# Where the raw weights of the next head pair are fetched to, and when the triangular inverse runs, in a hybrid RWKV-7 / FoX layer

## The chip, the cores and the metric

The kernel runs on one core of a Trainium2 chip. The metric is the device time of one execution in microseconds; the median of three executions of the kernel before is 1712.96 us (1705.19, 1712.96 and 1714.62 us).

Of the core's engines the text uses these names: PE is the matrix engine (PEld its weight loads), DVE the vector engine, ACT the scalar engine, POOL GpSimd, and SP the engine whose queue issues nearly all DMA transfers. Each engine works its queue in the order in which it stands.

## The reference, cut to what matters

One layer over 2048 positions of width 1024: a norm, one input projection, two branches (an RWKV-7 recurrence over 8 heads of 64, and attention with a forget gate over 8 heads), a gate, an output projection and a final norm.

```
h = rmsnorm(x, norm_g);  p = h @ w_in                      # 2048x1024 @ 1024x4232
p_rw, p_fox, gate = p[:, :1664], p[:, 1664:3208], p[:, 3208:]
# RWKV: r, k, v are 512 columns each; token shift, decay w, rate a, normalised kk
step:  sa    = state @ (-kk_t)
       state = state * w_t + sa (x) (kk_t * a_t) + v_t (x) k_t
       y_t   = state @ r_t
# FoX: softmax(q k^T / 8 + c_i - c_j, causal) @ v, with c the running sum of log_sigmoid(f)
y = concat(y_rw, y_fox) * silu(gate);  x = x + y @ w_out;  out = rmsnorm(x, final_g)
```

The kernel computes the recurrence in chunks of 64 positions: inside a chunk it needs the inverse of a unit lower triangular 64x64 matrix for each chunk and head.

## The kernel before, in words

**Stages.** Four blocks of 512 positions of x are loaded, normalised, transposed and split into a high and a low half-precision part (`load_x_block`). Then the main loop (L671 to L696) takes the RWKV heads in four pairs `p`, each over four blocks `b`. Attention, the chunk recurrence and the output projection follow; they are only started while the last projections run, and the change does not touch their code.

**A pair and a block.** For each block the loop projects r, k and v (`proj_T`, 24 matmuls of 512 columns each, L254), shifts them in time (`shifted`), and calls `prep`, a long chain over all engines: decay by a scan (L487), normalisation through PE (`ss`, L95 and L96), `rs`, `nk`, `k`, `th`, the pair of tiles `bk` and `ga` (L532 and L527), the matmuls `pb` and `pk` that multiply them (L541, L544), and masks that leave the triangular matrices in `mab`. Most results are stored to DRAM for the recurrence. After `prep`, `step(1)` writes one portion of the fillers.

**Fillers.** The attention projections (`fox_proj`, L332) and the gate projections (`gate_proj`, L254 with `pj_g`) do not depend on the pair loop. They are written as a generator in seven groups, f0, f1, f2, g0, g3, g6, f3, of which one portion is written after each block. PE uses them when the chain of `prep` is not ready.

**Weights.** A group of three 128-column tiles is fetched raw (32-bit, 512 KB each, L199) into tiles of the tag `wr`, of which there are three for the pairs and the fillers together. `prep_w` then takes the largest magnitude on DVE (`am`, L200), crosses partitions with two small PE operations (`over_partitions`, tile `px`), scales the tile on DVE (L216), rounds it on ACT (L218) and takes the remainder on POOL (L219). The rounded tiles of a pair (`wh_r`, `wl_r`) exist three times, so those of the next pair can only be written once the last block's projections have used the old ones. In the kernel before, `rw_weights(p + 1)`, fetch and conversion together, is written ahead of the projections of block 2 (`P_W` = 2).

**The inverse.** `inverse(p - 1, ...)` (L574) inverts the pair's triangular matrices on DVE: transposes into a tile `mu`, 60 small dependent operations on `tv` (L588, L590), transposes into `z` (32x64 per partition, 8 KB) and `ta` (same buffer as `mu`). `inverse_end` (L601) adds the off-diagonal blocks by small PE matmuls (L607, L615) with copies on ACT, and stores `z` to DRAM (L619). The first half is written after block 1 of the next pair (`P_INV` = 1), the second after block 2 (`P_END` = 2).

**Order.** The tile framework fixes the order in each engine's queue when the kernel is built: it plans all instructions on a modelled time line, in the order in which they are written where several could go, and an instruction written later may stand earlier in a queue if its inputs and its buffer are free earlier. On the chip that order then holds, whatever the real times are.

Of the kernel before, what the change touches and what calls it, by code (L numbers as in the profile page):

```python
# [9 lines left out]
F32 = mybir.dt.float32  # L10
# [20 lines left out]
NEG = -1e30  # L31
LN16 = math.log(16.0)
GS = 2048.0
P_W, P_INV, P_END = 2, 1, 2
N_A, N_B = 5, 20
VS = 2.0 ** -20
HR = ((0, 64), (64, 128))
# [2 lines left out]
def hymba_body(tc, x, norm_g, w_in, rw_mu, rw_w_up, rw_w0, rw_a_up, rw_a0, rw_k_k, rw_k_a, rw_r_k,  # L40
# [7 lines left out]
    with ctx:  # L48
# [140 lines left out]
            ts(isc[:, 0:n].bitcast(I32), e, 23, ALU.logical_shift_left)  # L189
            return sc  # L190

        def prep_w(n, offs, tag, outs, iall):

            nt = len(offs)
            am = wp.tile([128, 3, KT, 2], F32, name="am_" + n, tag="am")
            wrs = []
            for i, c0 in enumerate(offs):
                wr = wp.tile([128, KT, 128], F32, name=f"wr_{n}{i}", tag="wr", bufs=3)
                nc.sync.dma_start(wr, w_in[0, :, c0:c0 + 128].rearrange("(k p) n -> p k n", p=128))  # L199
                nc.vector.tensor_reduce(am[:, i].rearrange("q k g -> q (k g)"),  # L200
                                        wr.rearrange("q k (g c) -> q (k g) c", c=64), AX.X, ALU.max,
                                        apply_absolute_value=True)
                wrs.append(wr)
            a3 = am[:, 0:nt].rearrange("q i k g -> q (i k) g")
            nc.vector.tensor_tensor(a3, a3, gabx[:, 0:nt * KT].unsqueeze(2).to_broadcast([128, nt * KT, 2]), ALU.mult)
            mx = wp.tile([128, 6], F32, name="mx_" + n, tag="mx")
            nc.vector.tensor_reduce(mx[:, 0:2 * nt].rearrange("q (i g) -> q i g", g=2),
                                    am[:, 0:nt].rearrange("q i k g -> q i g k"), AX.X, ALU.max)
            ma = over_partitions(n, mx[:, 0:2 * nt], 2 * nt, wp, tag)
            sc = pow2_scale(n, ma, 2 * nt, wp, iall, tag)  # L210
            for i in range(nt):
                nc.vector.tensor_tensor(am[:, i], g_c.unsqueeze(2).to_broadcast([128, KT, 2]),
                                        sc[:, 2 * i:2 * i + 2].unsqueeze(1).to_broadcast([128, KT, 2]), ALU.mult)
            for i, (wr, (oh, ol)) in enumerate(zip(wrs, outs)):
                w3 = wr.rearrange("q k (g c) -> q (k g) c", c=64)
                nc.vector.tensor_tensor(w3, w3, am[:, i].rearrange("q k g -> q (k g)").unsqueeze(2)  # L216
                                        .to_broadcast([128, 2 * KT, 64]), ALU.mult)
                nc.scalar.activation(oh, wr, AF.Copy)  # L218
                nc.gpsimd.tensor_tensor(ol, wr, oh, ALU.subtract)  # L219

        def load_tiles(name, offs):

            iall = wp.tile([128, 6], F32, name="ia_" + name, tag="ia", bufs=2)
            ws = [(wp.tile([128, KT, 128], F16, name=f"wh_{name}{i}", tag="wh", bufs=3),
                   wp.tile([128, KT, 128], F16, name=f"wl_{name}{i}", tag="wl", bufs=3)) for i in range(len(offs))]
            prep_w(name, offs, "r", ws, iall)
            return ws, iall

        def load_w(name, offs, extra=None):

            wh = wp.tile([128, KT, 386], F16, name="fh_" + name, tag="fh", bufs=2)
            wl = wp.tile([128, KT, 386], F16, name="fl_" + name, tag="fl", bufs=2)
            iall = wp.tile([128, 6], F32, name="ja_" + name, tag="ja", bufs=2)
            cs = [slice(128 * i, 128 * i + 128) for i in range(len(offs))]
            prep_w(name, offs, "f", [(wh[:, :, c], wl[:, :, c]) for c in cs], iall)
            if extra is not None:
                for dst, src in ((wh, extra[0]), (wl, extra[1])):
                    nc.gpsimd.tensor_copy(dst[:, :, 384:386], src)
            return wh, wl, iall
# [143 lines left out]
        def group_w(i, fw):  # L383
            kind, n = groups[i]
            if kind == "f":
                c, fs = OFF_FOX + n * 128, slice(2 * n, 2 * n + 2)
                return load_w(f"f{n}", [c + j * 512 for j in range(3)], (fw[0][:, :, fs], fw[1][:, :, fs]))
            return load_w(f"g{n}", [OFF_GATE + (n + j) * 128 for j in range(min(3, 8 - n))])

        def fillers():  # L390

# [19 lines left out]
        with c1:  # L411
# [162 lines left out]
            def inverse(p, mab):  # L574

                mu = T(f"mu{p}", "mu", 1, (128, 32, 32))
                tv = T(f"tv{p}", "tv", 1, (128, 32, 32))
                nc.vector.transpose(mu.rearrange("q t s -> q (t s)"), mab[:, 0:32, :].rearrange("q t u -> q (t u)"))
                for q0 in (32, 96):
                    nc.vector.transpose(mu[q0:q0 + 32].rearrange("q t s -> q (t s)"),  # L580
                                        mab[q0:q0 + 32, 32:64, :].rearrange("q t u -> q (t u)"))
                nc.gpsimd.tensor_copy(tv, mu)
                nc.gpsimd.memset(tv.rearrange("q t j -> q (t j)")[:, 0:1024:33], 1.0)
                tm = T(f"tm{p}", "tm", 1, (128, 256))
                for s_ in range(1, 31):
                    r = 31 - s_
                    w = tm[:, 0:r * s_].rearrange("q (t j) -> q t j", j=s_)
                    nc.vector.tensor_tensor(w, mu[:, s_ + 1:32, s_:s_ + 1].to_broadcast([128, r, s_]),  # L588
                                            tv[:, s_:s_ + 1, 0:s_].to_broadcast([128, r, s_]), ALU.mult)
                    nc.vector.tensor_tensor(tv[:, s_ + 1:32, 0:s_], tv[:, s_ + 1:32, 0:s_], w, ALU.add)  # L590

                z = T(f"z{p}", "z", 1, (128, 32, 64))
                ta = T(f"ta{p}", "mu", 1, (128, 32, 32))
                nc.vector.transpose(z[:, :, 0:32].rearrange("q u t -> q t u"), tv)
                for q0 in (32, 96):
                    nc.vector.transpose(z[q0:q0 + 32, :, 32:64].rearrange("q u t -> q t u"), tv[q0:q0 + 32])
                    nc.gpsimd.memset(z[q0:q0 + 32, :, 0:32], 0.0)
                nc.vector.transpose(ta.rearrange("q u j -> q j u"), tv.rearrange("q t j -> q j t"))
                return partial(inverse_end, p, mab, z, ta)
# [19 lines left out]
                nc.sync.dma_start(d_z[p], z)  # L619

            load_x_block(0, sp, ps_r)
            whl, wll, iscl = load_w("l", [1536])
            with nc.allow_non_contiguous_dma("small parameter columns"):
                mu_c = pcol(rw_mu, 13, "mu_c")
            omu_c = derived("omu_c", mu_c, -1.0, ALU.mult, 1.0, ALU.add)
            sml, sol = mix_scales("l", iscl, 1, mu_c[:, 12:13], omu_c[:, 12:13])
            def rw_weights(p):
                ws, isc = load_tiles(f"r{p}", [i * 512 + p * 128 for i in range(3)])
                sm, so = mix_scales(f"r{p}", isc, 3, mu_c[:, p:p + 9:4], omu_c[:, p:p + 9:4])
                return ws, sm, so  # L630

            rw = [rw_weights(0)]
            uh = sp.tile([128, 2, 512], F32R, name="uh")
            ul = sp.tile([128, 512], F32R, name="ul")
            up = T("lup", "rs")
# [35 lines left out]
            for p in range(4):  # L671
                ws, sm, so = rw[p]
                mab = T(f"mab{p}", "mab", 2, (128, 64, 32))
                mabs.append(mab)
                for b in range(NB):
                    if p == 0:
                        ps = proj_T(f"l{b}", ps_mm.tile([128, TB], F32, name=f"pj_l{b}", tag="mm"), whl, wll, 0, b)
                        lw = low_rank_in(b, ps)
                    else:
                        lw = T(f"lw{p}_{b}", "lw", 1, (128, 2, TB), F32R)  # L680
                        nc.sync.dma_start(lw.bitcast(F32), d_l[b])
                    if b == P_W and p < 3:
                        rw.append(rw_weights(p + 1))
                    rkv = []
                    for i in range(3):
                        n = f"r{p}{b}{i}"
                        ps = proj_T(n, ps_mm.tile([128, TB], F32, name="pj_" + n, tag="mm"), *ws[i], 0, b)
                        o = T("sh_" + n, "sh" + "rkv"[i])
                        shifted(n, ps, 4 * i + p, sm[:, i:i + 1], so[:, i:i + 1], o)
                        rkv.append(o)  # L690
                    prep(p, b, *rkv, lw, mab)
                    step(1)
                    if p and b == P_INV:
                        end = inverse(p - 1, mabs[p - 1])
                    if p and b == P_END:
                        end()  # L696
            inverse(3, mabs[3])()


# [458 lines left out]
```

## Time and profile before

| | |
|---|---|
| median of three executions | 1712.96 us |
| the profiled execution | 1710.1 us |
| its span from the first to the last instruction | 1708.1 us |
| mean granted PE clock | 0.960 of full |
| PE busy | 1578.6 us, 92% |
| DVE busy | 1206.2 us, 71% |
| ACT busy | 839.1 us, 49% |
| POOL busy | 760.7 us, 45% |

All times in the rows are microseconds from the start of the span, unless they are marked ns. Busy PE time is matmul time, with pipelined matmuls overlapping; the granted clock says at which share of full speed PE ran in a stretch. The span is 2.0 us shorter than the profiled execution's time, and that execution is 2.9 us below the median.

### The profile page before, as it was taken

The numbers are of one execution on the slowest core, as the hardware profiler recorded it, in microseconds if no ns is written. First come the engines' busy times: TensorE is split into PE (matmuls) and PEld (weight loads), VectorE is DVE, ScalarE is ACT, GpSimd is POOL, SyncE is SP. The second block draws the span as 40 slices with busy tenths as digits, with TensorE's granted clock in tenths as the row PEclk, the third lists the DMA queues.
The fourth block names the chain that finished last, engine by engine and source line by source line (L and its number), as shares of the span: only waits on it lengthen the run. The fifth ranks groups of instructions, "written<-read, shape, count | busy, mean of one in ns | idle before, by whom it ended". The sixth has DMA issues, their size and how long they took to land. (4 is left out here: it accounts for less than half of the span.)

```text
span 1708.1 us, 36602 instructions
## 1 busy us (share of the span) xinstructions
PE 1578.6 (92%) x14182; PEld 977.1 (57%) x14182; DVE 1206.2 (71%) x2614; ACT 839.1 (49%) x1583; POOL 760.7 (45%) x838
## 2 busy tenths in 40 slices
PE   4999799999999999899999999899999998799998
PEld 2455355555555564445454566566666665577886
DVE  5975558975898669743844678588999997865443
ACT  5634444444434454445333247566676777465221
POOL 5643644445345543532201135455566666654000
PEclk9899899999999999999999999898999998899999
DMA  6422232323213242322225029766879632722452
GB/s 180 133 90 95 92 110 87 99 100 118 106 62 118 95 139 78 111 96 106 96 92 140 26 60 253 162 151 143 177 176 213 156 98 77 226 89 96 158 173 87
DMA packets 211982, 207.72 MB, mean 122 GB/s; under 512 B 53664, under 2 KB 173472, under 8 KB 211296
## 3 DMA queue, kind: packets, MB, share of 16 engines
q1 hardware_dynamic: 211808, 205.39, 42.0%
q8 instruction: 111, 1.82, 0.5%
q14 instruction: 63, 0.52, 0.1%
HBM read 123.34 MB, written 81.94 MB: 120 GB/s over the span
## 5 line engine op out<-in xcount | busy, mean ns | idle before, releaser
L1012 POOL TENSOR_TENSOR pl<-p,ph 128x512 f16<-128x512 f32 (+3 forms) x216 | 234.6, 1096 | 176.5 <-ACT ph L1010 71.2
L1006 ACT ACTIVATE p<-st,be 128x512 f32<-128x512 f32 (+1 forms) x320 | 193.3, 621 | 123.2 <-DVE pl L1012 32.9
L951 DVE TENSOR_REDUCE mx<-sq 128x1 f32<-128x384 f32 (+6 forms) x320 | 184.6, 601 | 21.6 <-PE sq L947 10.0
L332 PE MATMUL pf<-fh_f,hhi 128*128 128x386 f16 x512 | 170.3, 333 | 3.1 <-DVE fl L348 3.0
L332 PE MATMUL pf<-fl_f,hhi 128*128 128x386 f16 x512 | 169.1, 330 | 1.0 <-POOL fl_f L219 1.0
L332 PE MATMUL pf<-fh_f,hlo 128*128 128x386 f16 x512 | 169.4, 331 | 0.0
L254 PE MATMUL pj_r<-hhi,wh_r 128*128 128x512 f16 x384 | 147.5, 384 | 0.0
L254 PE MATMUL pj_r<-hlo,wh_r 128*128 128x512 f16 x384 | 147.3, 384 | 0.0
L254 PE MATMUL pj_r<-hhi,wl_r 128*128 128x512 f16 x384 | 146.8, 383 | 0.0
L341 POOL TENSOR_TENSOR fr<-ft,nhalf 128x4 f32<-128x4 f32 x64 | 65.9, 1030 | 177.9 <-DVE ft L101 171.8
L332 PEld LDWEIGHTS <-hhi 128*128 128x128 f16 x1024 | 99.5, 99 | 77.7 <-issue 13.4
L1016 PE MATMUL pv<-va,ph 128*128 128x65 f16 x1088 | 132.9, 197 | 8.1 <-DVE ot L1026 5.9
L1020 PE MATMUL pv<-va,pl 128*128 128x65 f16 x1088 | 129.7, 197 | 4.2 <-POOL pl L1012 2.2
L1018 PE MATMUL pv<-vb,ph 128*128 128x64 f16 x1088 | 132.0, 195 | 0.0
L1010 ACT ACTIVATE ph<-p 128x512 f16<-128x512 f32 (+3 forms) x220 | 121.2, 561 | 20.5 <-PE pv L1020 14.9
L999 PE MATMUL st<-qb,kb 68*128 68x512 f16 (+1 forms) x320 | 114.6, 361 | 10.3 <-DMA qb<-gl 10.0
L254 PEld LDWEIGHTS <-wh_r 128*128 128x128 f16 x768 | 75.0, 99 | 85.6 <-issue 6.0
L998 PE MATMUL st<-qa,ka 128*128 128x512 f16 (+1 forms) x320 | 114.2, 360 | 6.7 <-ACT p L1006 3.8
L947 PE MATMUL sq<-km,qb 66*128 66x384 f16 (+6 forms) x320 | 107.5, 355 | 10.4 <-DVE mx L951 5.2
L1016 PEld LDWEIGHTS <-ph 128*128 128x128 f16 x1088 | 102.9, 99 | 23.7 <-DVE ot L1026 7.0
L1020 PEld LDWEIGHTS <-pl 128*128 128x128 f16 x1088 | 102.6, 99 | 21.5 <-POOL pl L1012 5.2
L1018 PEld LDWEIGHTS <-ph 128*128 128x128 f16 x1088 | 102.9, 100 | 8.1 <-issue 1.2
(378 smaller groups left out, 4070.7 us busy)
## 6 DMA issues: line engine op xcount, KB each, us to landing
d_ga<-ga SPq DMA_DIRECT2D x32, 256.0 KB
d_gl<-gl SPq DMA_DIRECT2D x32, 256.0 KB
d_nk<-nkt SPq DMA_DIRECT2D x32, 256.0 KB
d_gate<-gv SPq DMA_DIRECT2D x32, 256.0 KB
G<-d_ga SPq DMA_DIRECT2D x32, 256.0 KB
G<-d_gl SPq DMA_DIRECT2D x32, 256.0 KB
NK<-d_nk SPq DMA_DIRECT2D x16, 512.0 KB
xr<-in_x_dram SPq DMA_DIRECT2D x16, 512.0 KB
```

Source lines behind the costliest of these rows:

```text
L254: nc.tensor.matmul(ps, a[:, kt, o:o + 128], h[:, kt, :], start=n == 0, stop=n == 3 * KT - 1)
L332: nc.tensor.matmul(ps, a[:, kt, js], w[:, kt, :], start=n == 0, stop=n == 3 * KT - 1)
L947: nc.tensor.matmul(ps[:, :w], qb[0:66, i * 128:i * 128 + 128], km[0:66, ks], start=True, stop=not last)
L951: nc.vector.tensor_reduce(mx[:, i, b:b + 1], ps[:, :w], AX.X, ALU.max)
L998: nc.tensor.matmul(ps[:, c0:], ka[:, k0:k0 + 128], qa[:, q0 + c0:q0 + 512], start=True, stop=False)
L999: nc.tensor.matmul(ps[:, c0:], kb[0:68, k0:k0 + 128], qb[0:68, q0 + c0:q0 + 512], start=False, stop=not diag)
L1006: nc.scalar.activation(p32[:, c0:], ps[:, c0:], AF.Exp, bias=be[:, j:j + 1])
L1010: nc.scalar.activation(ph[:, c0:], p32[:, c0:], AF.Copy)
L1012: eng.tensor_tensor(pl[:, c0:], p32[:, c0:], ph[:, c0:], ALU.subtract)
L1016: nc.tensor.matmul(pv[:, qq, 0:65], ph[:, s_], vh[:, j, 0:65], start=j == 0 and qq == 0, stop=False, skip_group_check=True)
L1018: nc.tensor.matmul(pv[:, qq, 0:64], ph[:, s_], vl[:, j], start=False, stop=False, skip_group_check=True)
L1020: nc.tensor.matmul(pv[:, qq, 0:65], pl[:, s_], vh[:, j, 0:65], start=False, stop=fin, skip_group_check=True)
```

## The change

The raw weights of pairs 1 to 3 are no longer fetched into `wr` tiles. They go into two tiles that share the buffers of the inverse: two of the three into one of the tag `z`, the third into one of the tag `mu`. The three fetches are written at the end of block 2 (`P_F` = 2), the conversion ahead of block 3's projections (`P_W` = 3). So that these buffers are free, the inverse of the pair before is written after block 0 (`P_INV` = 0) and its second half after block 1 (`P_END` = 1). Pair 0, the fillers and the inverse of pair 3 keep their places; the fillers now have the three `wr` tiles to themselves once pair 0 is loaded. The functions are split so that fetch and conversion can be written apart; what they compute is the same.

```diff
-P_W, P_INV, P_END = 2, 1, 2
+P_F, P_W, P_INV, P_END = 2, 3, 0, 1
...
-        def prep_w(n, offs, tag, outs, iall):
-
-            nt = len(offs)
+        def fetch_w(n, offs, tiles=None):
+
+            wrs = tiles or [wp.tile([128, KT, 128], F32, name=f"wr_{n}{i}", tag="wr", bufs=3) for i in range(len(offs))]
+            for wr, c0 in zip(wrs, offs):
+                nc.sync.dma_start(wr, w_in[0, :, c0:c0 + 128].rearrange("(k p) n -> p k n", p=128))
+            return wrs
+
+        def prep_w(n, wrs, tag, outs, iall):
+
+            nt = len(wrs)
             am = wp.tile([128, 3, KT, 2], F32, name="am_" + n, tag="am")
-            wrs = []
-            for i, c0 in enumerate(offs):
-                wr = wp.tile([128, KT, 128], F32, name=f"wr_{n}{i}", tag="wr", bufs=3)
-                nc.sync.dma_start(wr, w_in[0, :, c0:c0 + 128].rearrange("(k p) n -> p k n", p=128))
+            for i, wr in enumerate(wrs):
                 nc.vector.tensor_reduce(am[:, i].rearrange("q k g -> q (k g)"),
...
-            def rw_weights(p):
-                ws, isc = load_tiles(f"r{p}", [i * 512 + p * 128 for i in range(3)])
+            def rw_fetch(p, tiles=None):
+                return fetch_w(f"r{p}", [i * 512 + p * 128 for i in range(3)], tiles)
+
+            def rw_weights(p, wrs):
+                ws, isc = load_tiles(f"r{p}", wrs)
                 sm, so = mix_scales(f"r{p}", isc, 3, mu_c[:, p:p + 9:4], omu_c[:, p:p + 9:4])
                 return ws, sm, so
 
-            rw = [rw_weights(0)]
+            rw = [rw_weights(0, rw_fetch(0))]
...
                     if b == P_W and p < 3:
-                        rw.append(rw_weights(p + 1))
+                        rw.append(rw_weights(p + 1, wnext))
...
                     if p and b == P_END:
                         end()
+                    if p < 3 and b == P_F:
+                        w2 = T(f"wz{p}", "z", 1, (128, 2, KT, 128))
+                        w1 = T(f"wm{p}", "mu", 1, (128, KT, 128))
+                        wnext = rw_fetch(p + 1, [w2[:, 0], w2[:, 1], w1])
```

The calls of `load_w` for the fillers change only in form: `fetch_w` stands directly inside them.

## Rows read from the trace of the kernel before

**Rows 1.** Busy time by stage; x counts instructions, PEclk is the granted clock.
```profile
100.00:780.00 680.00, 636.64 (x4321) 351.87 (x4320) 476.69 (x1054) 301.13 (x570) 316.85 (x382) 0.96 0.29 99
...
946.00:1020.00 74.00, 72.34 (x483) 44.30 (x481) 53.92 (x173) 23.00 (x59) 18.89 (x23) 1.00 0.13 40
```

**Rows 2.** The same columns, for three stretches around the weight conversions of pairs 1, 2, 3.
```profile
186.60:202.50 15.90, 4.50 (x39) 2.80 (x39) 11.53 (x19) 5.63 (x8) 7.88 (x11) 0.57 0.33 100
342.00:357.00 15.00, 12.70 (x74) 6.61 (x73) 13.72 (x32) 2.01 (x6) 7.97 (x9) 0.77 0.20 62
530.00:545.00 15.00, 11.59 (x70) 6.22 (x69) 14.62 (x31) 2.42 (x6) 6.97 (x9) 0.77 0.34 104
```

**Rows 3.** PE and DVE queues in order of time, 186 to 198 us.
```profile
186.22 0.40 PE L96 MATMUL ss<-la,bones 128*128 128x512 f32 x1
...
187.34 1.22 DVE L200 TENSOR_REDUCE am_r<-wr_r 128x16 f32<-128x1024 f32 x1 [9.72 <-DMA wr_r<-in_w_in_dram]
188.48 0.68 DVE L101 TENSOR_SCALAR rs<-ss 128x512 f32<-128x512 f32 x1
...
193.05 1.21 DVE L200 TENSOR_REDUCE am_r<-wr_r 128x16 f32<-128x1024 f32 x1
...
198.01 0.48 PE L541 MATMUL pb<-ga,bk 64*64 64x128 f32 x2 [11.40 <-DVE bk L532]
```

**Rows 4.** DVE in order of time, 346 to 350 us.
```profile
346.86 1.21 DVE L200 TENSOR_REDUCE am_r<-wr_r 128x16 f32<-128x1024 f32 x1
...
348.98 0.74 DVE L532 SCALAR_TENSOR_TENSOR bk<-th,eI 128x256 f32<-128x256 f32 x2
```

**Rows 5.** DVE, then PE, in order of time, 533 to 536 us.
```profile
533.01 1.20 DVE L200 TENSOR_REDUCE am_r<-wr_r 128x16 f32<-128x1024 f32 x1
534.14 0.94 DVE L532 SCALAR_TENSOR_TENSOR bk<-th,eI 128x256 f32<-128x256 f32 x1
...
535.22 0.51 PE L541 MATMUL pb<-ga,bk 64*64 64x128 f32 x5 [1.87 <-DVE bk L532]
```

**Rows 6.** POOL and SP in order of time: release of wr tiles, fetches into them.
```profile
181.34 6.10 POOL L219 TENSOR_TENSOR fl_f<-wr_f,fh_f 128x1024 f16<-128x1024 f32 x3
...
183.43 4.40 SPq L199 DMA_DIRECT2D wr_r<-in_w_in_dram  x3
...
523.28 0.38 SPq L199 DMA_DIRECT2D wr_r<-in_w_in_dram  x1
```

**Rows 7.** All instructions on the raw pair weights: ns min/median/max, then first and last start.
```profile
L200 DVE TENSOR_REDUCE am_r<-wr_r x12: 1202/1206/1220, 25.5 to 536.9; 128x16 f32<-128x1024 f32 x12
L216 DVE TENSOR_TENSOR wr_r<-wr_r,am_r x12: 1205/1214/1219, 47.0 to 557.9; 128x1024 f32<-128x1024 f32 x12
```

**Rows 8.** Columns of Rows 1, for the stretches between the scans (L487) of blocks.
```profile
325.10:372.30 47.20, 44.90 (x276) 25.41 (x274) 39.78 (x91) 20.59 (x40) 27.05 (x28) 0.93 0.36 118
372.30:419.30 47.00, 45.39 (x324) 25.65 (x324) 24.98 (x57) 23.35 (x47) 22.99 (x26) 0.93 0.34 113
...
564.30:607.70 43.40, 42.27 (x265) 23.29 (x263) 26.32 (x56) 20.62 (x38) 23.64 (x26) 0.96 0.32 98
```

**Rows 9.** POOL, SP, PE and DVE in order of time, 416 to 449 us.
```profile
416.29 2.14 POOL L219 TENSOR_TENSOR wl_r<-wr_r,wh_r 128x1024 f16<-128x1024 f32 x1 [1.25 <-ACT wh_r L218]
...
434.95 0.38 SPq L619 DMA_DIRECT2D d_z<-z  x1
...
446.86 0.38 PE L254 MATMUL pj_r<-hhi,wh_r 128*128 128x512 f16 x1
...
447.51 1.23 DVE L578 STREAM_TRANSPOSE mu<-mab 128x1024 f32<-128x1024 f32 x1
```

**Rows 10.** POOL's remainder of a weight group, then one small DVE operation twice.
```profile
332.71 6.10 POOL L219 TENSOR_TENSOR fl_f<-wr_f,fh_f 128x1024 f16<-128x1024 f32 x3
...
334.89 1.92 DVE L101 TENSOR_SCALAR ft<-ft 128x4 f32<-128x4 f32 x1
...
352.80 0.17 DVE L101 TENSOR_SCALAR ft<-ft 128x4 f32<-128x4 f32 x1
```

More of the change, by code (lines that the diff above doesn't have):

```diff
@@ L202, in prep_w @@
                                         apply_absolute_value=True)
-                wrs.append(wr)
             a3 = am[:, 0:nt].rearrange("q i k g -> q (i k) g")
@@ L219, in prep_w, with load_tiles, load_w @@
                 nc.gpsimd.tensor_tensor(ol, wr, oh, ALU.subtract)
-        def load_tiles(name, offs):
+        def load_tiles(name, wrs):
             iall = wp.tile([128, 6], F32, name="ia_" + name, tag="ia", bufs=2)
             ws = [(wp.tile([128, KT, 128], F16, name=f"wh_{name}{i}", tag="wh", bufs=3),
-                   wp.tile([128, KT, 128], F16, name=f"wl_{name}{i}", tag="wl", bufs=3)) for i in range(len(offs))]
-            prep_w(name, offs, "r", ws, iall)
+                   wp.tile([128, KT, 128], F16, name=f"wl_{name}{i}", tag="wl", bufs=3)) for i in range(len(wrs))]
+            prep_w(name, wrs, "r", ws, iall)
             return ws, iall
-        def load_w(name, offs, extra=None):
+        def load_w(name, wrs, extra=None):
             wh = wp.tile([128, KT, 386], F16, name="fh_" + name, tag="fh", bufs=2)
@@ L233, in load_w @@
             iall = wp.tile([128, 6], F32, name="ja_" + name, tag="ja", bufs=2)
-            cs = [slice(128 * i, 128 * i + 128) for i in range(len(offs))]
-            prep_w(name, offs, "f", [(wh[:, :, c], wl[:, :, c]) for c in cs], iall)
+            cs = [slice(128 * i, 128 * i + 128) for i in range(len(wrs))]
+            prep_w(name, wrs, "f", [(wh[:, :, c], wl[:, :, c]) for c in cs], iall)
             if extra is not None:
@@ L386, in group_w @@
                 c, fs = OFF_FOX + n * 128, slice(2 * n, 2 * n + 2)
-                return load_w(f"f{n}", [c + j * 512 for j in range(3)], (fw[0][:, :, fs], fw[1][:, :, fs]))
-            return load_w(f"g{n}", [OFF_GATE + (n + j) * 128 for j in range(min(3, 8 - n))])
+                return load_w(f"f{n}", fetch_w(f"f{n}", [c + j * 512 for j in range(3)]), (fw[0][:, :, fs], fw[1][:, :, fs]))
+            return load_w(f"g{n}", fetch_w(f"g{n}", [OFF_GATE + (n + j) * 128 for j in range(min(3, 8 - n))]))
         def fillers():
@@ L621, in hymba_body @@
             load_x_block(0, sp, ps_r)
-            whl, wll, iscl = load_w("l", [1536])
+            whl, wll, iscl = load_w("l", fetch_w("l", [1536]))
             with nc.allow_non_contiguous_dma("small parameter columns"):
```

## The prediction

> **What bounds the kernel now.** I read the stages first [rows 1]. In the pair loop (100 to 780 us) PE is busy 636.64 of 680 us, DVE 476.69; from 946 to 1020 us, where the fillers end, PE is busy 72.34 of 74. So PE is the bound up to 1020 us, and as fillers can take any free PE time there, a change of the loop is worth the PE idle time and the slow clock that it takes out of it. There are 680 - 636.6 = 43.4 us of idle time, and a mean granted clock of 0.96.
>
> Next the three stretches in which the pair weights are converted [rows 2]. PE idles 15.9 - 4.5 = 11.4, 15 - 12.7 = 2.3 and 15 - 11.59 = 3.4 us, and the granted clock falls to a mean of 0.57, 0.77 and 0.77, which mixes full speed (2.4 GHz) with stretches at 1.2 GHz. Work at the lower level costs half of its time: at most 4.5 / 2 = 2.3 us in the first, and 15 x 0.23 = 3.45 us in each of the others. The three lose 11.4 + 2.3, 2.3 + 3.45 and 3.4 + 3.45: 13.7, 5.75 and 6.85, together 26.3 us. That is the most that taking the conversion away could give back there.
>
> Last, who is late. For pair 1, DVE stands 9.72 us before its first reduction, waiting for the transfer; `rs`, next in its queue, was ready when `ss` ended at 186.62 and starts at 188.48 [rows 3]. At 346.86 and 533.01 there is no wait, but a reduction of 1.2 us lies just ahead of `bk`, for which PE stands idle [rows 4, 5].
>
> **The fetch.** Before, it waits for a `wr` tile: it starts at 183.43, when POOL has finished the first of three filler tiles (181.34 + 6.10 / 3 = 183.37), and SP spends 4.40 us on three issues as the others come free [rows 6]. That `wr` was the limit shows again at 523.28, where one fetch goes out alone. Under the change pair 1's fetch waits for nothing later than the x blocks loaded ahead of the loop, so it lands long before its reduction. What goes is not 9.72 us, as DVE had nothing else ready for most of them: it is 188.48 - 186.62 = 1.86 us of `rs`, and the 1.21 us of the reduction at 193.05, which stands in the same chain [rows 3]. 3.1 us. The remaining 8.3 us of the gap stay: the chain through ACT and POOL from `ss` to `bk` is late then, and the fillers' order decides whether PE has work. The nine transfers stay as many and as large.
>
> For pairs 2 and 3 the fetch waits for the store of `z`, `d_z`. Now it goes out at 434.95 [rows 9]; `inverse_end` moves one block forward, a block being 47.0 or 43.4 us [rows 8], so about 389. Behind a waiting fetch stand SP's stores of `ga` and `gl`, and behind those POOL and DVE, which refill them. The nearest row for that wait is the 4.40 us above: 0 to 4.4 us a pair, and as the same wait is taken out elsewhere, below nothing too, down to -4.4. I take 0.
>
> **The conversion.** On DVE it is three reductions of 1.206 and three scalings of 1.214 us [rows 7], 7.3 us a pair, the small operations left out. For pair 2 it leaves a stretch in which DVE is busy 39.78 of 47.2 us and enters one with 24.98 of 47.0, so with 22.0 us free; for pair 3 the new stretch has 43.4 - 26.3 = 17.1 free [rows 8]. Where it leaves, the reductions ahead of `bk` go, and with them the short gaps and the fall of the clock behind them: 5.75 and 6.85. Where it enters, it stands ahead of another block's `rs` and `bk`. The price is between 0 (free DVE time covers it) and the same 12.6 us again. With DVE at 53 to 61% there, not 84%, I take a third: 4 us. The ACT and POOL work stays: it waited for block 3's projections before and does after.
>
> Does it come too late? Pair 2's last remainder ends at 416.29 + 2.14 = 418.4, its first projection starts at 446.86, and the first transpose into `mu` at 447.51 [rows 9]: 28 and 29 us of slack. From a fetch at about 392, some 3.9 us to the first reduction (183.43 to 187.34 [rows 3, 6]), two more reductions (2.4), 21.0 from the last reduction to the last scaling (557.9 - 536.9 [rows 7]) and 2.14 on POOL end it at about 421. The added wait of the inverse for `mu` is then over before it starts; behind it DVE's block-0 work would stand.
>
> **The inverse.** It is written after block 1, yet starts at 447.51, ahead of pair 2's block 0 projections' results: the planner starts it as soon as the last `mab` is there [rows 9]. Writing it earlier can't start it sooner; it changes rank only against block 1's work. PE idles 47.2 - 44.9 = 2.3 us in such a stretch [rows 8], so three pairs give at most 6.9 us, and I bound the loss by the same. I take 0, for it and for `inverse_end`, whose work is the same a block earlier.
>
> **The fillers** get their three `wr` tiles sooner. PE is full where they convert [rows 1], so 0.
>
> One row speaks against moving the conversion towards the inverse: a DVE operation of 0.17 us takes 1.92 while POOL runs a weight remainder (332.71 to 338.81), 1.75 us more [rows 10]. The Trainium skill (SBUF — State Buffer, "Who interferes with whom") has DVE instructions with two SBUF inputs blocked for a whole instruction by a GpSimd instruction that reads SBUF, and the other way round. By that, three remainders among the inverse's operations could hold DVE for their whole length; the trace agrees in kind, as 1.75 lies within 6.10 / 3 = 2.03. What it would make of the time is the third rival.
>
> **Sum.** 3.1 + 5.75 + 6.85 - 4 = 11.7 us. From the profiled execution's 1710.1 (span 1708.1 and 2.0 around it) that makes 1698.4; this execution lies 2.9 under the median of the runs, so 1701.3. I forecast 1701 us, with a range of its own of 1694 to 1709.
>
> **The rivals.**
>
> 1. The price moves along with the work: the reductions hold up block 3's chain as they held up block 2's, and only pair 1's 3.1 us are won: 1709.9. For: they are written ahead of block 3's projections, so they rank above its chain. Against: the free DVE time there.
>
> 2. The other side: the buffers of the inverse close a circle. The fetch waits for `d_z`, the conversion for the fetch, the next inverse for the conversion. If `inverse_end` stays near where it is (434.95), the same 29.4 us end at 464.4, 17.5 us after 446.86. It decides from a delay of 28 us on. Where the planner foresaw this, fillers cover it and it costs nothing; where it didn't, PE stands 17.5 us and loses 3.45 to the clock. One such boundary, with the mean gain of one pair (6.3) left: 17.5 + 3.45 - 3.1 - 6.3 = +11.5, so 1724.5; both would give 35 + 6.9 - 3.1, so 1752. For: the chain is new, and the transfer can't start before the store has landed. Against: `inverse_end` has all its inputs a block earlier.
>
> 3. The conversion slides some 29 us, and its remainders fall among the inverse's operations: three holds of 1.75 us for two pairs, 10.5 us of the 11.7: 1711.8. By the whole-length blocking of the Trainium skill (SBUF — State Buffer) it would be an estimated 3 x 2.14 x 2 = 12.8, so 1714.
>
> 4. More than forecast: the relieved DVE lets the whole of the three stretches close: 26.3, so 1686.7.
>
> That the change doesn't do what it says is part of rival 1: if pair 1's fetch still stands late in SP's queue, even the 3.1 are gone.
>
> **How the numbers follow.** What a measurement of this kernel tells from no change is about 0.5%, 8.6 us: faster is under 1704.4, slower over 1721.5. The forecast has 0.45, of which 0.33 lie under 1704.4 and 0.12 above. Rival 1 has 0.18 (0.01 faster, 0.16 within, 0.01 slower), rival 2 0.18 (0.03 within, 0.15 slower), rival 3 0.07 (0.06 within, 0.01 slower), rival 4 0.12, all faster. Faster 0.33 + 0.01 + 0.12 = 0.46, within 0.12 + 0.16 + 0.03 + 0.06 = 0.37, slower 0.17. The range takes in rival 4 with 2.7 us of the inverse's bound, from 1684, and rival 2 with one late boundary, to 1726. The two ends leave out 0.04 and 0.08.
>
> **What would show it.** Right: pair 1's fetch no longer behind the fillers' remainder, and no DVE wait for it; no reduction of pair weights between `nk` and `bk` of block 2; a granted clock near 1.0 where the conversions of pairs 2 and 3 had 0.77; pair 2's and 3's reductions in the next stretch, with PE idle there by no more than before; the first transpose into `mu` still a few us after the last `mab`. Wrong: PE waiting for ACT or POOL at a pair's first projection (rival 2), new gaps before `pb` in block 3 (rival 1), inverse operations of over 1 us beside POOL's remainders (rival 3). I am wrong altogether if PE's idle time in the loop is not under 43.4 us.

## The result and the profile after

The changed kernel takes 1722.9 us (median of 7 runs, 1716.93 to 1727.53), the kernel before 1705.6 us in the same session (7 runs, 1701.6 to 1714.62): ratio 1.0079 on record, 95% interval 1.0056 to 1.0102 (the plain quotient of the two medians is 1.0101). It is slower, where I forecast 1701 us and faster.

In the loop the change gained, and more than I forecast. The windows of the changed kernel, same columns as [rows 1, 2, 8]:

```profile
100.00:780.00 680.00, 646.02 (x4652) 357.88 (x4650) 493.01 (x1075) 318.28 (x597) 333.10 (x388) 0.98 0.30 102
946.00:1020.00 74.00, 73.84 (x626) 46.78 (x624) 55.93 (x168) 31.34 (x72) 27.15 (x29) 1.00 0.14 41
...
186.60:202.50 15.90, 15.71 (x110) 8.73 (x109) 12.93 (x29) 6.32 (x12) 8.76 (x10) 1.00 0.11 42
335.00:350.00 15.00, 15.00 (x106) 9.10 (x106) 10.98 (x34) 5.09 (x13) 7.36 (x9) 0.89 0.30 108
518.00:533.00 15.00, 13.96 (x100) 8.65 (x101) 12.23 (x36) 4.99 (x13) 7.92 (x10) 0.89 0.37 119
...
560.00:607.00 47.00, 44.68 (x342) 25.25 (x342) 36.63 (x84) 22.54 (x44) 28.79 (x29) 1.00 0.36 124
372.00:419.00 47.00, 44.66 (x390) 25.91 (x387) 34.81 (x77) 22.59 (x43) 25.20 (x24) 1.00 0.36 118
```

PE's idle time from 100 to 780 us falls from 43.4 to 34.0 us, and the granted clock rises from 0.96 to 0.98. The stretch of pair 1's conversion, 11.4 us of idle time at a mean clock of 0.57 before [rows 2], now holds 110 matmuls instead of 39, is full and at 2.4 GHz. The stretches that the conversions of pairs 2 and 3 left lie some 7 and 12 us earlier now, at 335 and 518 us: better than before, but not clean, with 0.0 and 1.0 us of idle time (2.3 and 3.4 before) and a clock of 0.89 (0.77 before). The stretches that took in the conversions of pairs 2 and 3 carry some 10 us more DVE work each than before [rows 8] and have their full clock.

The steps of the change, in order of time: SP, DVE, SP again, POOL, DVE of the changed kernel.

```profile
94.27 0.39 SPq L196 DMA_DIRECT2D wz<-in_w_in_dram  x1
...
99.42 0.37 SPq L196 DMA_DIRECT2D wm<-in_w_in_dram  x1
...
137.81 2.33 DVE L204 TENSOR_REDUCE am_r<-wz 128x16 f32<-128x1024 f32 x2
...
381.98 0.41 SPq L622 DMA_DIRECT2D d_z<-z  x1
386.25 1.43 SPq L196 DMA_DIRECT2D wz<-in_w_in_dram  x2
...
413.90 2.12 POOL L222 TENSOR_TENSOR wl_r<-wm,wh_r 128x1024 f16<-128x1024 f32 x1
...
442.85 1.24 DVE L581 STREAM_TRANSPOSE mu<-mab 128x1024 f32<-128x1024 f32 x1
```

Pair 1's fetch goes out at 94 us instead of 183 [rows 6] and its reductions stand at 138 instead of 187 [rows 3]. The store of `z` is at 382 (434.95 before, forecast 389), pair 2's last remainder ends at 416.0 (forecast 421), and `mu` follows at 442.85, 27 us later [rows 9].

The time is lost behind the loop, in code that the change does not touch. For the kernel before, and then for the changed one, first two lines by tile, which give the start of the first and the last such matmul: `pf`, the fox projections, and `pX`, the first product in each step of the chunk recurrence (the chain). Then three windows: up to the first `pX`, from the first to the last, and from there to the 256th of 768 output matmuls (`po`, at 1579.7 and 1597.5).

```profile
L332 PE MATMUL pf<-fh_f,hlo x512: 324/325/528, 89.0 to 1020.1; 128*128 128x386 f16 x171
L737 PE MATMUL pX<-SV,G x512: 222/222/366, 1034.0 to 1417.2; 128*64 128x64 f32 x171
```

```profile
790.00:1034.00 244.00, 236.04 (x1801) 128.02 (x1798) 147.81 (x398) 91.60 (x167) 52.64 (x57) 0.99 0.32 94
1034.00:1417.20 383.20, 359.54 (x5539) 246.35 (x5538) 334.01 (x716) 257.44 (x491) 228.59 (x231) 0.96 0.72 166
1417.20:1579.70 162.50, 144.88 (x1549) 105.71 (x1544) 115.51 (x184) 95.45 (x185) 91.92 (x77) 0.94 0.40 125
```

```profile
L335 PE MATMUL pf<-fh_f,hlo x512: 324/325/528, 91.6 to 1021.7; 128*128 128x386 f16 x171
L747 PE MATMUL pX<-SV,G x512: 222/222/369, 1036.2 to 1434.0; 128*64 128x64 f32 x171
```

```profile
790.00:1036.20 246.20, 232.81 (x1707) 126.44 (x1705) 157.40 (x415) 95.82 (x176) 58.34 (x61) 0.97 0.29 83
1036.20:1434.00 397.80, 371.89 (x5469) 255.45 (x5470) 328.81 (x697) 254.69 (x483) 226.81 (x228) 0.91 0.67 159
1434.00:1597.50 163.50, 140.57 (x1413) 100.08 (x1409) 111.91 (x171) 85.21 (x169) 85.30 (x70) 0.93 0.41 123
```

The lead of the loop is gone at the last fox projection (1021.7 against 1020.1), and the chain then takes 397.8 us instead of 383.2, at a granted clock of 0.91 instead of 0.96. (The changed kernel's profile is of its slowest execution, 1727.53 us.) The two kernels have the same instructions there, 10,655 of them, but the planner gave them another order on every engine: it puts 68 matmuls of the attention maxima (`sq`) and 22 of the scores (`st`) ahead of the last fox projection, against 49 and 8 in the kernel before. (The expectations below give these counts twice as high, as weight loads were counted with them.)

### The profile page after: what moved, and what is told of

It is laid out like the page before. It is cut to its first block, busy times and chain, and to the rows that moved or that the text cites. A ratio compares the mean times of both kernels' runs of the same rounds, so it can differ in the third digit from the quotient of the medians.

```text
span 1725.8 us, 36574 instructions
## 1 busy us (share of the span) xinstructions
PE 1592.4 (92%) x14182; PEld 983.8 (57%) x14182; DVE 1220.8 (71%) x2614; ACT 840.2 (49%) x1583; POOL 771.9 (45%) x838
## 5 line engine op out<-in xcount | busy, mean ns | idle before, releaser
L1026 PE MATMUL pv<-va,ph 128*128 128x65 f16 x1088 | 140.0, 200 | 16.3 <-DVE ot L1036 12.0
L1028 PE MATMUL pv<-vb,ph 128*128 128x64 f16 x1088 | 139.7, 198 | 0.0
L1030 PE MATMUL pv<-va,pl 128*128 128x65 f16 x1088 | 136.3, 199 | 2.2 <-POOL pl L1022 1.9
L957 PE MATMUL sq<-km,qb 66*128 66x384 f16 (+6 forms) x320 | 115.8, 376 | 18.4 <-DMA km<-d_nc 11.0
L1020 ACT ACTIVATE ph<-p 128x512 f16<-128x512 f32 (+3 forms) x220 | 119.8, 561 | 24.4 <-PE pv L1030 13.9
L1008 PE MATMUL st<-qa,ka 128*128 128x512 f16 (+1 forms) x320 | 118.2, 373 | 9.4 <-ACT p L1016 5.1
L1026 PEld LDWEIGHTS <-ph 128*128 128x128 f16 x1088 | 105.5, 101 | 33.9 <-DVE ot L1036 12.8
L1009 PE MATMUL st<-qb,kb 68*128 68x512 f16 (+1 forms) x320 | 118.7, 374 | 2.5 <-DMA qb<-gl 2.5
L1028 PEld LDWEIGHTS <-ph 128*128 128x128 f16 x1088 | 105.8, 102 | 10.6 <-issue 4.4
```

The lines of the kernel that those rows point to most:

```text
L1008: nc.tensor.matmul(ps[:, c0:], ka[:, k0:k0 + 128], qa[:, q0 + c0:q0 + 512], start=True, stop=False)
L1009: nc.tensor.matmul(ps[:, c0:], kb[0:68, k0:k0 + 128], qb[0:68, q0 + c0:q0 + 512], start=False, stop=not diag)
L1020: nc.scalar.activation(ph[:, c0:], p32[:, c0:], AF.Copy)
L1026: nc.tensor.matmul(pv[:, qq, 0:65], ph[:, s_], vh[:, j, 0:65], start=j == 0 and qq == 0, stop=False, skip_group_check=True)
L1028: nc.tensor.matmul(pv[:, qq, 0:64], ph[:, s_], vl[:, j], start=False, stop=False, skip_group_check=True)
L1030: nc.tensor.matmul(pv[:, qq, 0:65], pl[:, s_], vh[:, j, 0:65], start=False, stop=fin, skip_group_check=True)
```

## The experiments

**1. The loop and the later order, crossed.** Theory 1: the loop's gain is real, and the new order of the untouched stage costs more than it. To separate the two, the order of the later stage is held: every instruction from the first of the attention stage on gets an ordering edge to the one that follows it on its engine in the other kernel's order. Instructions, data and waits stay.

```diff
+def pin_order(tc):
...
+    for e, n in PIN_N:
+        order = np.cumsum(d[at:at + n])
+        at += n
+        cand = per[e][-n:]
+        for a, b in zip(order, order[1:]):
+            tc.add_manual_dep(cand[b], cand[a].name, info, reason="pin")
...
         hymba_body(tc, *args)
+        pin_order(tc)
```

The changed loop with the later order of before (pin_after):

> The changed kernel, with every engine's order of the instructions of attention, chain and output projection (10,655 of them) held to the order that they have in the kernel before; the loop and the fox projections keep the changed kernel's order. Theory 1 (the loop's gain of some 12 us is real, and the planner's new order of the later stage, which the change does not touch, loses some 30 us): 12 us under the kernel before, ratio 0.990 to 0.996, and the time from the last fox projection on is the kernel before's within 5 us. Theory 2 (attention heads that start earlier against the chain lose whatever the order, as their loads then stand behind the chain's on SP): no gain, ratio 1.00 to 1.01, with waits of over 3 us on km and qb loads before 1.2 GHz stretches between 1040 and 1420 us.

The loop of before with the changed kernel's later order (pin_before):

> The kernel before, unchanged in its loop, with the instructions of attention, chain and output projection held to the order that the changed kernel gives them. Theory 1: the order alone costs some 30 us, ratio 1.012 to 1.022. Theory 2 (it is the early start, not the order): the same as the kernel before within 0.4%, ratio 0.996 to 1.004.

Measured, each against the kernel before in its own session (median, ratio, interval):

| | later order of before | later order of the changed kernel |
|---|---|---|
| loop of before | 1710.64, 1 | 1750.71, 1.0236 (1.0214 to 1.0257) |
| changed loop | 1685.44, 0.9861 (0.9841 to 0.9881) | 1722.9, 1.0079 (1.0056 to 1.0102) |

Theory 1 holds, and both effects are larger than it said. The changed loop is worth 1.4% with the one order and 1.0079 / 1.0236 = 0.985, so 1.5%, with the other: 24 to 26 us. The order costs 2.4% with the one loop and 1.0079 / 0.9861 = 1.022 with the other: 38 to 40 us. Within the intervals (0.2 to 0.3% each) they add up. Theory 2, that the early start hurts whatever the order, is out: with the order of before the early start is kept to the end, as the same two views of pin_after show.

```profile
L339 PE MATMUL pf<-fh_f,hlo x512: 324/325/528, 91.2 to 999.4; 128*128 128x386 f16 x171
L751 PE MATMUL pX<-SV,G x512: 222/222/366, 1013.3 to 1396.6; 128*64 128x64 f32 x171
```

```profile
790.00:1013.30 223.30, 215.19 (x1498) 115.69 (x1496) 139.29 (x383) 82.76 (x152) 48.07 (x52) 0.98 0.30 87
1013.30:1396.60 383.30, 360.22 (x5537) 246.90 (x5536) 334.20 (x716) 257.70 (x490) 227.86 (x231) 0.96 0.72 166
1396.60:1558.60 162.00, 144.90 (x1551) 105.20 (x1546) 116.82 (x184) 95.34 (x185) 91.63 (x77) 0.94 0.41 125
```

Last fox projection, first and last `pX`: each 20.6 or 20.7 us earlier than before, and the chain again 383.3 us long.

Two things are not held apart by this. What is called the loop here is the changed loop with the order that the planner gave it; that order was never held. And no kernel was held to its own order unchanged, to see what the added edges do by themselves. That they do little is suggested by the times: each order keeps its own, within 3 us, whichever loop stands ahead of it and whether it is held or planned: from the first `pX` to the last output matmul 666.5 us (kernel before) and 666.0 (pin_after) in the one, 682.0 (changed kernel) and 679.1 (pin_before) in the other.

The windows of pin_after also say where the 38.9 us between pin_after and the changed kernel (last output matmul at 1679.3 and 1718.2) lie. Count, as the prediction did, the idle time and the stretch times (1 - clock). Up to the first `pX`: 8.1 + 4.5 = 12.6 us here, 13.4 + 7.4 = 20.8 there. The chain: 23.1 + 15.3 = 38.4 here, 25.9 + 35.8 = 61.7 there. After it: 17.1 + 9.7 = 26.8 here, 22.9 + 11.5 = 34.4 there. That is 8.2 + 23.3 + 7.6 = 39.1 us. (The first `pX` comes 22.9 us later; by this count 14.7 of these are attention work that is only done earlier.) PE's work is the same; the bad order has it stop for 13.9 us more, and the other 25 are lost to 1.2 GHz.

**2. One part of the change alone.** fetch_only is the changed kernel with the inverse back in its place, inv_only the kernel before with the inverse moved. Both orders are the planner's own.

```diff
-P_F, P_W, P_INV, P_END = 2, 3, 0, 1
+P_F, P_W, P_INV, P_END = 2, 3, 1, 2
...
-P_W, P_INV, P_END = 2, 1, 2
+P_W, P_INV, P_END = 2, 0, 1
```

> The fetch into the inverse's buffers at block 2 and the conversion at block 3, with the inverse left in block 1 of the next pair. Theory 1: PE's idle time between 100 and 780 us is 34 to 37 us (43.4 before), the projections of the fox stage run 8 to 12 us earlier, and the total goes by whatever order the later stage gets, not by the loop. Theory 3 (one part of the change costs the loss by itself): if the fetch is that part, ratio 1.005 to 1.010; if not, 0.990 to 0.997.

> The kernel before with the inverse of a pair in block 0 of the next one (its end in block 1), the weights fetched and converted at block 2 as before. Theory 1: PE's idle time between 100 and 780 us stays 43 us within 3, the fox stage is reached at the same time within 4 us, and a change of the total of over 5 us comes from 1036 to 1440 us. Theory 3: if the moved inverse is what costs, ratio 1.005 to 1.018 with the time lost in the loop; if not, 0.996 to 1.004.

Measured: fetch_only 1726.53 us, 1.0106 (1.0086 to 1.0126); inv_only 1726.48 us, 1.0076 (1.0046 to 1.0105). The loop in fetch_only, then in inv_only:

```profile
100.00:780.00 680.00, 629.85 (x4288) 349.87 (x4286) 481.40 (x1059) 300.57 (x567) 317.45 (x377) 0.95 0.29 98
100.00:780.00 680.00, 637.94 (x4550) 354.15 (x4548) 478.62 (x1058) 305.58 (x578) 323.35 (x382) 0.96 0.30 99
```

Of the fetch alone theory 1 had the loop wrong. PE's idle time in the loop is 50.1 us (43.4 before), and its last fox projection is at 1033.8, 13.7 us late; from there it loses no more in the chain (381.0 us). From SP, PE's weight loads, POOL and DVE of fetch_only:

```profile
418.12 0.32 SPq L622 DMA_DIRECT2D d_z<-z  x1
...
422.03 1.01 SPq L196 DMA_DIRECT2D wz<-in_w_in_dram  x2
...
422.09 0.96 PEld L544 LDWEIGHTS pb<-ga,bk 64*64 64x64 f32 x10 [7.27 <-POOL bk L536]
...
444.51 2.12 POOL L222 TENSOR_TENSOR wl_r<-wm,wh_r 128x1024 f16<-128x1024 f32 x1
...
414.94 1.22 DVE L204 TENSOR_REDUCE am_r<-wm 128x16 f32<-128x1024 f32 x1 [2.04 <-DMA wm<-in_w_in_dram]
...
416.92 0.75 DVE L508 SCALAR_TENSOR_TENSOR nk<-sh_r,kk_c,rs 128x512 f32<-128x512 f32 x1 [0.76 <-ACT rs L501]
...
623.62 1.22 DVE L204 TENSOR_REDUCE am_r<-wz 128x16 f32<-128x1024 f32 x1 [3.06 <-DMA wz<-in_w_in_dram]
```

With the inverse where it was, the fetch waits for `d_z` until 422, and the remainder ends at 446.6, 30 us later than in the changed kernel. Right behind the inverse's last products, which are done at 415.0, PE waits 7.2 us for `bk`, with 17 us at 1.2 GHz around it; between 606 and 628 us three waits of 3.6, 2.7 and 3.5 us come with another 17, from 603 on. Only the last of these hangs on the fetch as the rows show it: DVE waits 3.06 us for `wz`, and PE then 3.5 us for the largest magnitude `mx_r`. The 7.2 us are not traced to it: `nk`, ahead of `bk`, last waited for ACT (until 416.9), when DVE's reduction of `wm` was over (416.2). So the fetch pays together with the inverse's move and loses without it, but by which of these waits, and how much of it is the order that the planner gave this loop, is open.

The inverse alone leaves the loop as it was (idle 42.1 us); with 56 `sq` and 14 `st` ahead it has its last fox projection 5.9 us late and its last output matmul 12.6 us late (1713.1 against 1700.5). Theory 1 expected that loss in the chain; the chain takes 384.3 us, only 1.1 more than before. Of the 12.6 us 8.1 are there at the first `pX` and 3.4 come behind the last.

Either part alone is slower by about as much as both together, as theory 3 had it for a guilty part; but the fetch alone loses in the loop, where the changed kernel gains, and the inverse alone loses behind it. Neither is the changed kernel's loss by itself.

**3. Which stretch of the order.** Two mixed orders on the changed loop: mix_ba takes before's order up to the first `pX` and then the changed kernel's, mix_ab the reverse.

```diff
-order = order_before
+head = order_before[:first_pX]                                  # mix_ba
+order = head + [i for i in order_changed if i not in head]
```

> The changed kernel's loop; the later stage in the order of the kernel before up to the first product of the chain of states (pX), and from there in the changed kernel's order, without what has been done by then. Theory 1a (the loss of 39 us lies in two places: 23 us of it because 203 more TensorE instructions of attention are issued ahead of the chain's start and push it back, 16 us in the order of the chain's loads and steps after it): ratio 0.992 to 0.998, 1697 to 1707 us, the first pX at 1013 us as with the held order of before, and 12 to 18 us lost after it. Theory 1b (all of the loss follows from the late start): 1685 us within 5, ratio 0.983 to 0.989.

> The changed kernel's loop; the later stage in the changed kernel's order up to the first product of the chain (first pX at 1036 us, 203 more TensorE instructions done by then), and from there in the order of the kernel before, without what has been done by then. Theory 1a (the chain sets the stage, attention done early gives nothing back): 1705 to 1712 us, ratio 0.997 to 1.001, the chain from first to last pX 380 us or more. Rival (TensorE's work is only moved; what is done early is given back as there is less beside the chain): 1685 to 1692 us, ratio 0.985 to 0.989, the chain from first to last pX 360 to 368 us.

Measured: mix_ba 1713.04 us, 1.0014 (1.0001 to 1.0027), above its range; mix_ab 1706.59 us, 0.9988 (0.9970 to 1.0007), as theory 1a had it, but not for its reason. In mix_ba the first `pX` did not come at 1013 but at 1034.9: the attention work that the changed kernel's order wants ahead of the chain was still written first in what followed. So mix_ba does not test what it was made for. In mix_ab, the longest of PE's waits in the chain, and the chain's window:

```profile
PE st L1013 <- DMA qb<-gl: 23.1, 2, 20.7
```

```profile
1030.70:1414.60 383.90, 343.58 (x5333) 237.58 (x5335) 319.07 (x685) 243.48 (x467) 218.01 (x222) 0.94 0.71 165
```

PE is busy for 343.6 us in the chain, 16.6 less than in pin_after: the attention done early is given back, against theory 1a. The chain is no shorter all the same: the seam of the two orders makes a wait of 20.7 us of its own, without which it would be some 363 us, as the rival has it (an estimate, 383.9 - 20.7). That early attention is a loss by itself is not shown.

**4. Other orders of the planner.** The changed kernel with later fillers written ahead of attention's second start, nothing held.

```diff
-N_A, N_B = 5, 20
+N_A, N_B = 16, 9
...
-N_A, N_B = 5, 20
+N_A, N_B = 8, 17
```

> The changed kernel with eleven of the twenty later filler steps written ahead of the second pair of attention steps (N_A, N_B = 16, 9), nothing held. The planner now puts 102 score matmuls of the maxima and 8 of the scores ahead of the last fox projection (98 and 16 in the kernel before, 136 and 44 in the changed one). Theory 1a: with the attention back behind the fox projections the first pX comes at 1010 to 1017 us, and the total is 1683 to 1700 us, ratio 0.984 to 0.994. Rival (the count says nothing, each planned order is a draw of its own): anywhere from 0.984 to 1.02, with no early first pX needed for a short time.

> The changed kernel with N_A, N_B = 8, 17, nothing held: the planner puts 112 matmuls of the maxima and 28 of the scores ahead of the last fox projection, between the kernel before and the changed one. Theory 1a: the first pX at 1018 to 1026 us, the total 1690 to 1710 us, ratio 0.988 to 1.000. Rival (each order is a draw of its own): outside of it.

Measured: na16_after 1696.59 us, 0.9917 (0.9895 to 0.9939), first `pX` at 1007.7; na8_after 1703.49 us, 0.9957 (0.9940 to 0.9975), first `pX` at 1021.3. Totals in both ranges, one start 2 us early. Both beat the kernel before, with the changed kernel's loop. The count ranks the orders only roughly: na16_after has the fewest scores ahead (4) and is slower than pin_after (8). Its early start doesn't shorten what follows: from the first to the last `pX` it takes 400.2 us, more than the changed kernel. And na8_after has the same counts as inv_only (56 `sq`, 14 `st`), yet a chain of 382.7 us and a gain. The ranges were wide, so the rival, a draw for each order, is not out.

**5. The loads in the queue.** The waits of PE in the chain, in the changed kernel and in pin_after:

```profile
PE sq L957 <- DMA km<-d_nc: 6.3, 2, 3.1
PE pY L773 <- DVE SV L760: 2.6, 3, 1.1
PE sq L957 <- DMA qb<-d_gs: 2.6, 1, 2.6
PE st L1009 <- DMA qb<-gl: 2.5, 1, 2.5
```

```profile
PE st L1013 <- DMA qb<-gl: 9.6, 2, 7.2
PE sq L961 <- DVE mx L965: 2.4, 3, 1.7
```

In the changed kernel three waits, for small loads that stand behind the chain's loads on SP, are each followed by a stretch at 1.2 GHz: 3.1 us by 17.1, 3.2 by 10.3, 2.6 by 13.6. The first of these stretches, and one of 13.6 us that has no such load ahead of it but a wait of 1.4 us for `mx`:

```profile
1055.30:1072.40 17.10, 16.89 (x137) 10.44 (x138) 9.88 (x21) 7.18 (x14) 5.12 (x6) 0.50 0.80 194
...
1219.20:1232.80 13.60, 13.53 (x126) 9.22 (x126) 9.07 (x19) 5.74 (x12) 5.76 (x7) 0.50 0.64 142
```

The first of two kernels holds the changed kernel's order and moves seven of the small transfers forward on SP; the second holds before's order and moves four 512 KB loads back behind `qb<-gl`:

```diff
 SP's order around pair 3 in pinA_loads
+d_nc<-nch
+d_nc<-nch
 G<-d_ga
...
-d_nc<-nch
+km<-d_nc
+km<-d_nc
 NK<-d_nk
...
 SP's order in pin_gate_late
-bo<-d_bo
-gg<-d_gate
-bo<-d_bo
-gg<-d_gate
 d_yf<-ot
...
 km<-d_nc
+bo<-d_bo
+gg<-d_gate
+bo<-d_bo
+gg<-d_gate
```

> The changed kernel with its own order held on every engine; on SP alone seven small transfers are moved ahead of 4 to 13 of the chain's loads: the two stores of d_nc of pair 2 and of pair 3, the two km rows of head 6 that come from d_nc, and the qb rows of head 7 that come from d_gs. Theory 4 (of the 39 us that the order loses, most are three waits of the maxima's matmuls for these loads, 3.1, 3.2 and 2.6 us, with the 17.1, 10.3 and 13.6 us at 1.2 GHz that follow them): two of the waits go and the first is shorter, the time at 1.2 GHz between first and last pX falls from 72 to 35 to 50 us, and the total by 13 to 22 us against the changed kernel, ratio to the kernel before 0.995 to 1.001. Rival (the waits only move; other instructions hold the chain in the same stretches): total within 5 us of the changed kernel, ratio 1.005 to 1.010.

> The changed kernel's loop with the later stage in the order of the kernel before, and on SP alone the first four loads of bo and gg (512 KB each) moved behind the loads of the second pair of heads. There TensorE waits 7.2 us for the rows qb<-gl, which are ready at 1041.7 and issued at 1048.1, with the 16 DMA engines full. Theory 4: that wait falls under 3 us, the 10.3 us at 1.2 GHz behind it shrink too, and the total is 5 to 11 us under that of the held order, ratio to the kernel before 0.979 to 0.984. Rival (the loads are late for want of bandwidth, whatever their order; the group norm or the chain's SV loads wait in its place): within 3 us of the held order, ratio 0.984 to 0.988.

Measured: pinA_loads 1715.91 us, 1.0042 (1.0025 to 1.0060), between the two expectations. The window of its chain, and the first line of PE's waits in it:

```profile
1034.40:1420.70 386.30, 359.85 (x5469) 248.65 (x5470) 331.74 (x697) 254.02 (x483) 228.71 (x228) 0.94 0.70 164
```

```profile
PE sq L961 <- DMA km<-d_nc: 5.7, 2, 3.5
```

By the windows 26.4 + 23.2 = 49.6 us are lost in it, against 61.7; but the changed kernel's profile is of an execution 4.6 us above its median, and by the ratios the gain is 0.4%, some 6 of 39 us. One of the three waits is gone and one shorter (2.2 us); the first, 3.5 us, stayed. So the seven transfers carry a small part of the loss (by the intervals 1 to 11 us); the rest is not assigned.

pin_gate_late takes 1683.87 us, 0.9863 (0.9836 to 0.9890). The wait that it aims at, in order of time from pin_after (SP, then PE):

```profile
1031.30 1.48 SPq L786 DMA_DIRECT2D bo<-d_bo  x1
...
1048.14 0.55 SPq L991 DMA_DIRECT2D qb<-gl  x1
...
1055.66 0.61 PE L1013 MATMUL st<-qb,kb 68*128 68x512 f16 x1 [7.15 <-DMA qb<-gl]
```

is gone: in pin_gate_late the longest wait for `qb<-gl` in the chain is 2.4 us, and the chain is 376.4 us long instead of 383.3. The ratio is no better than the 0.9861 of pin_after and lies in the rival's range, not in theory 4's. The profiled execution is 5.6 us shorter (span 1681.4 against 1687.0), but these two executions took 1683.18 us, 0.7 under the median of their kernel, and 1688.7, 3.3 over it: a gain in the total is not shown. Both are faster than either kernel of this case.

**6. SP's order alone.** Only SP's order is held to before's; the planner sets the other engines.

```diff
-PIN_N = [('Activation', 841), ('DVE', 1316), ('PE', 7632), ('Pool', 369), ('SP', 497)]
+PIN_N = [('SP', 497)]
```

> The changed kernel with only SP's order of the later stage held to the kernel before's; the planner orders the other engines itself (it puts 104 matmuls of the maxima and 16 of the scores ahead of the last fox projection). If the queue of loads is what makes an order good or bad: within 6 us of the fully held order, ratio 0.983 to 0.990. If the order on TensorE, VectorE, ScalarE and GpSimd matters by itself: ratio 0.990 or more.

Measured: 1695.37 us, 0.9925 (0.9900 to 0.9951): some 1.5 of the 2.2% between the orders come back, not all of it. That SP's queue brought them is not shown: the planner drew a new order for the other engines with it (52 `sq` and 8 `st` ahead), and na16_after, with nothing held, has 0.9917. What it shows is that before's order on SP is not enough for before's later stage.

## Why the prediction was wrong

**The step that failed** is the one that carries the loop's gain to the end: "PE is the bound up to 1020 us ... a change of the loop is worth the PE idle time and the slow clock that it takes out of it", from which the sum went straight to the total. It prices everything behind the loop at nothing. The planner orders all instructions in one pass over modelled time, and an earlier loop gave it another order for the 10,655 instructions behind; that order costs 38 to 40 us (experiment 1). Even with the later order of before, the forecast's own range from 1694 us is missed from below (0.9861 of 1712.96 is 1689). No rival had the order; rival 2, which came out near the measured time (1724.5), has another mechanism, and it did not happen: `mu` waits for nothing at 442.85.

**The terms.** Forecast for the loop 11.7 us; with the order held it gives 24 to 26 us by the ratios and 20.7 at the last fox projection. Too small was pair 1's term: 3.1 us, as "the remaining 8.3 us of the gap stay". They did not stay; the stretch is full at 2.4 GHz, so all but 0.2 of the 13.7 us went. Somewhat too large were the terms of pairs 2 and 3: their old stretches still lose 1.7 and 2.7 us, so some 4.1 and 4.2 went, not 5.75 and 6.85. Too dear was the price at the new place: 4 us were taken. In the two stretches idle time grew by 0.7 and 1.2 us [rows 8], but the clock rose from 0.93 and 0.96 to 1.00, so they lose less than before. Counted like the prediction, the loop lost 43.4 + 27.2 = 70.6 us before and 34.0 + 13.6 = 47.6 after: 23.0 us, where the rounding of each clock leaves 3.4 us either way. Rival 4 (all three stretches close, 26.3 us, 1686.7) has the size of what the loop did, and its mechanism for pair 1 alone; it had a chance of 0.12. That its time is within 2 us of pin_after's is in part luck.

**The inverse and the fetch** went as worked out: the first half starts 4.7 us sooner, and the conversions of pairs 2 and 3 end 27 and 26 us ahead of `mu`. DVE does wait for the transfers into `wm`, 1.9 us for each of the two pairs; what that costs is not shown. That the inverse's move is worth 0 missed what it is there for: without it, the fetch costs 13.7 us up to the last fox projection (experiment 2). Rival 2's circle shows at the inverse's old place, at a fraction of its price: in fetch_only PE waits 0.4 us for the last remainder of pair 2 and 3.5 us for `mx_r` of pair 3, where the rival had 17.5 us for each. Rival 3 had nothing to act on, as the remainders end ahead of `mu`; its row [rows 10] is of an operation with one tensor input, so it doesn't bear on the rule on two inputs that is cited with it.

**The test that I named**, idle time in the loop under 43.4 us, was passed while the kernel got slower: it looked only at the stage that I had argued about. Of the signs for being right, the clock near 1.0 at the old places of pairs 2 and 3 did not come (0.89).

## What to carry to other kernels

Where a planner fixes the order when the kernel is built, a change in one stage can draw a new order for every stage behind it, as it did here. Compare the order of the untouched stages first, and put their spread into the range: with one and the same loop, five orders (the changed kernel, pin_after, na16_after, na8_after, spB_free) gave 0.986 to 1.008 here. Judge a local change with the later order held, and when it is a gain, keep a good order with it: that gave 1685 us, 1.4% under the kernel before.

## What the runs showed of the hardware

- A pause of PE can cost more by the clock than by itself: in the changed kernel pauses of 3.1, 2.5, 3.2 and 2.6 us in the chain were followed by 17.1, 10.2, 10.3 and 13.6 us at 1.2 GHz, of which half is lost. The length of the pause does not tell the price: 1.4 us had 13.6 us behind it, 2.0 us had 3.4, and in pinA_loads 3.5 us had 10.2 where 3.1 had 17.1. The mean clock of 0.91 in the chain is worth 35.8 us, the idle time 25.9.
- A 4 KB load can be late by large ones ahead of it in SP's queue: in pin_after `qb<-gl` was issued at 1048.14, behind 2 MB of loads issued from 1031 to 1037 among others, and PE had it at 1055.66. With these moved behind it, it was issued at 1043.95 and PE had it at 1050.80; no wait over 2.4 us for such a load is left in the chain. The time from issue to use hardly changed (7.5 and 6.9 us); what the four cost was the issue, for which SP spent 1.0 to 1.5 us on each there and 0.4 to 0.5 us at their later place.
